# A two-layer decoder's MLPs on one core: M2 behind the whole of M1, product by product over all chunks, and M1's f tiles as half products

## The chip, the core and the metric

One core of a Trainium2 chip runs the whole program. The metric is the device time of one launch in microseconds; a kernel is timed in several runs, and the median counts. The profile is of one further execution, with a span from the first to the last instruction and the busy time of each engine: PE (matmuls), PEld (weight loads of PE), DVE, ACT, POOL, and SP, which only issues DMAs here.

## What is computed

A decoder of two layers on 512 tokens of width 1024, all in float32. Layer 0 mixes by pooling, layer 1 by a gated spatial unit (SGU); both then have the same MLP, which is where the change is:

```python
def sq_relu_mlp(h, w1, w2):
    return jnp.square(jax.nn.relu(h @ w1)) @ w2

for i in range(DEPTH):
    mod = c_act @ ada_w[i] + ada_b[i]
    sh1, sc1, g1, sh2, sc2, g2 = jnp.split(mod, 6, axis=-1)
    h = modulate(rmsnorm(x, norm_mix_g[i]), sh1, sc1)
    ...
    x = x + g1[:, None, :] * y
    h = modulate(rmsnorm(x, norm_mlp_g[i]), sh2, sc2)
    x = x + g2[:, None, :] * sq_relu_mlp(h, mlp_w1[i], mlp_w2[i])
return rmsnorm(x, final_g)
```

`w1` is 1024 x 4096 and `w2` 4096 x 1024. The first product is called M1 here, its 4096 columns are 32 f tiles of 128, four chunks of 8; the second product is M2, and a chunk is 1024 of its contraction rows.

## The kernel before

**Precision.** A float32 operand is split in a high and a low part (`split`, L168, for weights: one ACT copy and one DVE subtract on 128 x 1024; `parts`, L596, for activations). Each product is three matmuls, low x high, high x low and high x high (`mm3`, L180, whose matmul stands in L186). A PE matmul has 128 x 128 weights and 256 or 512 columns.

**Seven for eight.** A product of 2 x 2 blocks is done with seven block products instead of eight, in a form with four accumulators: `ORDER = (1, 5, 6, 3, 7, 2, 4)` names them; 1, 6, 7, 4 go into one accumulator (X), 5 and 3 into another (Z), 2 stands alone. Four of the seven operands on either side are sums of blocks. On the weight side the sums form a chain in one tile: B11, then B12, B22 and B21 are added in turn (`CHAIN`, for products 5, 6 and 4); product 7 takes B12 with B22 added.

**How M1 goes.** In layer 0 a sweep over the eight k tiles (L549 to L575) does 7 f tiles in seven PSUM banks while the activations are still being normed; the other 25 are dense, one `f_run` (L648) each, of 24 matmuls with 512 columns. In layer 1 the first 8 are dense, in halves of 256 tokens, and the other 24 go as `s` units (`s_run`, L730): for each quarter of a chunk pair `(c, j)`, 4 f tiles, seven half products of 24 matmuls with 256 columns. The chain's steps 5 and 6 are added by DVE (L712), step 4 and product 7's block by DMA issued from POOL with an accumulating write (L707). The sums on the activation side are made in four steps by `a_sums` (L662).

**How M2 goes.** Chunks 0 to 2 each take seven products, `p` units (`p_prep` L776, `p_run` L847) of 24 matmuls with 512 columns; every product's banks are evicted and added to y in SBUF by DVE (L867) or copied by ACT. The chain is added by DVE in layer 0 (L790 on, `by_dma` false), by POOL's DMAs in layer 1 (L773). Chunk 3 is dense: eight `q` units (L895) of 24 matmuls.

**The order.** PE's order is written out by hand: a list of units (L913 to L925), in which the p units of chunk c stand between the M1 units of chunk c + 1. Before a unit runs, the operands of some units ahead are prepared (`ahead`, L933). DVE, ACT, POOL and SP get their orders from a scheduler, by the program's order and the buffers. Weight blocks pass through three raw tiles of 4 KB a partition (`w4`) and five pairs of split tiles (`wts`). `extra` spreads the ada tiles over the units: 56 loads of 512 KB with one DVE multiply-and-sum each (L206), which give the modulation of later stages.

**Layer ends.** `gated` (L967) takes a token tile's result into x and sums squares, `normed` (L988) norms two token tiles, turns them on PE (L1000) and splits them. In layer 1, x is written to DRAM (`spill`) and read back through POOL's queue (`reload`, L1017) to make room.

**Matmuls split in columns.** `HEAD` and `TAIL` (L78) split some first or last matmuls of a unit in layer 1 in two column ranges, where s and p units meet. `SHIFT`, `BASE` and `GAP` move tiles by words within 128.

Of the kernel before, what the change touches and what calls it, by code (L numbers as in the profile page):

```python
# [7 lines left out]
F32 = mybir.dt.float32  # L8
# [6 lines left out]
P = 128  # L15
# [11 lines left out]


LINE = 128
SHIFT = {"o": 64, "q": 0, "g": 0}  # L30

BASE = 32
# [45 lines left out]
HEAD = {1: {0: 32}, 5: {0: 64}, 6: {0: 128}, 3: {0: 224}, 4: {0: 128, 1: 128, 2: 128}}  # L78
TAIL = {7: {2: 256}, 2: {2: 448}}


@with_exitstack
def decoder_kernel(ctx: ExitStack, tc: tile.TileContext, xtok, vecs, rows, fgrow, ada0, adag, ada1, pool_w, w1s, w1, w1f, w1b, w2, w2e, w_v, w_u, w_o, wsT, lnp, bs, out):
# [44 lines left out]
    GAP = 16  # L128
    shift(big, BASE - GAP)

    def hparts(gap):
        t = big.tile([P, 2 * KD * S + GAP], F32R, name="hb", tag="hb")
        return t[:, GAP - gap : GAP - gap + 2 * KD * S].rearrange("p (h k s) -> p h k s", h=2, k=KD)

    h_ = [hparts(0)]

    shift(big, LINE - GAP)
    x_ = [big.tile([P, 2, D], F32, name=f"x{h}", tag=f"x{h}") for h in range(2)]
    shift(big, GAP)
    cb = big.tile([P, D], F32, name="cb")  # L140
    gb = big.tile([P, D], F32, name="gb")
# [4 lines left out]
    def H(k, c):  # L146

        return h_[0][:, 0, k, c], h_[0][:, 1, k, c]
# [8 lines left out]
    def raw4(src):  # L157
        r = w4.tile([P, D], F32, name="raw", tag="w4")
        nc.sync.dma_start(r, src)
        return r  # L160
# [51 lines left out]

    dram = ctx.enter_context(tc.tile_pool(name="dram", bufs=1, space=bass.MemoryType.DRAM))
# [10 lines left out]


# [13 lines left out]
    with (  # L239
# [205 lines left out]
        xf = st.tile([P, KD, S], F32, name="xf")  # L445
# [20 lines left out]
        def turned(g):  # L466
            for k in (2 * g, 2 * g + 1):
                A.activation(xf[:, k], pxs.pop(k), AF.Copy)
# [33 lines left out]
        ht, rbs = {}, []  # L502
# [20 lines left out]
        def norm_hi(k):  # L523
            t = ht[k] = st2.tile([P, S], F32, name="ht", tag="ht")
            V.scalar_tensor_tensor(t, xf[:, k], scl[0][1][:, k : k + 1], rbs[0], ALU.mult, ALU.mult)
            A.activation(H(k, ALL)[0], t, AF.Identity, bias=mod(0, c_sh(1, k)))

        def norm_lo(k):
            h, l = H(k, ALL)
            V.scalar_tensor_tensor(l, ht.pop(k), mod(0, c_sh(1, k)), f32(h), ALU.add, ALU.subtract)  # L530
# [20 lines left out]
        for k in range(KD):  # L551
# [12 lines left out]
            else:  # L564
                norm_lo(k)
            (xh, xl), (wh, wl) = H(k, ALL), wk[k][1:]
# [12 lines left out]
    vy = ctx.enter_context(tc.tile_pool(name="vy", bufs=1))  # L579

    def ytile(name):
        return vy.tile([P, NT, D], F32, name=name, tag="y")

# [6 lines left out]

    def parts(o, a):  # L596

        A.activation(o[0], a, AF.Copy)
        V.tensor_tensor(o[1], a, f32(o[0]), ALU.subtract)

    def mlp(i, first, extra, last, ending):

        with (
            tc.tile_pool(name="gq", bufs=3) as gq,
            tc.tile_pool(name="su", bufs=1) as su,
            tc.tile_pool(name="pad0", bufs=1) as pad0,
            tc.tile_pool(name="op", bufs=2) as op,
            tc.tile_pool(name="pad1", bufs=1) as pad1,  # L610
            tc.tile_pool(name="w2p", bufs=3) as w2p,
            tc.tile_pool(name="hx", bufs=1) as hx,
        ):
            shift(pad0, SHIFT["o"])
            shift(pad1, SHIFT["q"] - SHIFT["o"])
            g, y_ = {}, []

            def y(t, dh):
                if not y_:
                    y_.append(ytile("y"))  # L620
                return y_[0][:, t, S * dh : S * dh + S]

            def square(t):
                A.activation(t, t, AF.Square)

            def new_g(c, j):
                g[c, j] = gq.tile([P, 4, S], F32, name="g", tag="g")

            def put(f, po):

                c, q = divmod(f, 8)
                j, p = divmod(q, 4)
                if p == 0:
                    new_g(c, j)
                t = g[c, j][:, p]
                A.activation(t, po, AF.Relu)  # L636
                square(t)

            def quad(c, r, j):

                return g[c, j].rearrange("p a (h r t) -> p a h r t", h=2, r=2)[:, :, :, r]


            def f_prep(u):
                c, f = u
                return split(raw4(w1[8 * c + f] if i == 0 else w1f[8 * c + f]))

            def f_run(u, w):  # L648
                c, f = u
                po = bank("po")  # L650
                wv = w[0].rearrange("p (k c) -> p k c", k=KD), w[1].rearrange("p (k c) -> p k c", k=KD)
                n = 256 if i else S
                for t in range(0, S, n):
                    for k in range(KD):
                        mm3(po[:, t : t + n], cut(wv, ALL, k), H(k, slice(t, t + n)), k == 0, k == KD - 1)
                put(8 * c + f, po)

            sums_a = {}  # L660

            def a_sums(step):  # L662
# [599 lines left out]
```

## Time and profile before

| | us |
|---|---|
| median of 3 runs | 871.62 |
| lowest, highest run | 870.48, 875.11 |
| span of the profiled execution | 867.7 |
| PE busy in it | 854.0 |
| DVE busy | 667.7 |
| ACT busy | 448.4 |
| POOL busy | 49.5 |

The profile's own time is its span; a run's time is measured around the launch. The stages by the chain of waits: loads, ada tiles and the pooling mixer to about 60 us; the sweep to 99; layer 0's M1 and M2 to 395; the SGU to 540; layer 1's M1 and M2 to 858; then the last norm and the output. Groups of the profile's instructions are read as: line, engine, operation, output <- inputs, count | busy us, mean ns of one | idle time before them and what ended it. In the chain, a row is start, length and what it was; `po` is a bank of M1 or the SGU, `pm` of M2, `px` a turned block. For a DMA the row has the issuing queue, count, size and median time from issue to landing; q1 is the queue of plain loads, q0 that of the DMAs issued from POOL.

### The profile page before, as it was taken

To read this page: it belongs to the slowest core of one execution; us is meant where nothing else is said; L and a number is where in the kernel's file an instruction comes from. 1 tells how busy PE (TensorE), PEld (TensorE's weight loads), DVE (VectorE), ACT (ScalarE), POOL (GpSimd) and SP (SyncE) were. 2 spreads that over 40 slices of the span, in tenths; PEclk is the share of its full clock that TensorE was granted. 3 is DMA by queue.
4 is the path that set the end of the run, shared out by engine and by line. 5 is a ranking of instruction groups with operands and counts; after the bars stand their busy time and mean duration, and the time that the engine had idled before them with its cause. 6 is when DMAs were issued, how large, how long until landed. Compare 5 with 4: busy or idle time off the path is not lost.

```text
span 867.7 us, 11816 instructions
## 1 busy us (share of the span) xinstructions
PE 854.0 (98%) x4595; PEld 737.5 (85%) x4595; DVE 667.7 (77%) x884; ACT 448.4 (52%) x653; POOL 49.5 (6%) x69
## 2 busy tenths in 40 slices
PE   8999999999999999999999999999999999999996
PEld 6778888888888888888888888999999998999885
DVE  5889697788869886657799766676687697779855
ACT  4285755454444445238333326665775576566521
POOL 3000000000000000000020001011101000100001
PEclk9999999999999999999999999999999999999999
DMA  9959746454455341605757426937678587668302
GB/s 349 417 217 327 272 172 215 168 181 140 179 205 170 124 168 49 218 27 216 249 186 245 170 74 215 340 75 171 166 240 190 144 232 217 146 147 266 123 24 97
DMA packets 40045, 163.39 MB, mean 188 GB/s; under 512 B 4507, under 2 KB 4659, under 8 KB 34742
## 3 DMA queue, kind: packets, MB, share of 16 engines
q1 hardware_dynamic: 35282, 137.72, 43.8%
q0 software_dynamic: 4560, 24.66, 13.7%
q8 instruction: 36, 0.59, 0.3%
q10 hardware_dynamic: 148, 0.27, 0.1%
q14 instruction: 19, 0.16, 0.1%
HBM read 158.42 MB, written 4.21 MB: 187 GB/s over the span
## 4 chain that ended last, share of the span: by engine, by line
PE 91%; DMA 4%; DVE 2%; ACT 1%; issue 1%; SPq 0%; POOLq 0%; POOL 0%; DVEq 0%; ACTq 0%
PE po L186 52%; PE pm L186 36%; DMA wh<-in_ada 2%; DMA wl<-in_ada 1%; DMA ada<-in_adag 1%; PE po L1104 1%; ACT sq L279 1%; PE px L1000 1%; PE po L570 0%; PE po L573 0%; PE po L571 0%; DVE wl L174 0%; DVE tmp L972 0%; DVE h L1007 0%; PE px L464 0%
## 5 line engine op out<-in xcount | busy, mean ns | idle before, releaser
L186 PE MATMUL po<-hb,wh 128*128 128x256 f32 (+1 forms) x1252 | 298.9, 332 | 0.0
L186 PEld LDWEIGHTS po<-hb,wh 128*128 128x128 f32 x1252 | 211.5, 188 | 23.5
L186 PE MATMUL po<-hb,wl 128*128 128x256 f32 (+2 forms) x632 | 209.0, 333 | 0.4 <-DVE wl L174 0.4
L174 DVE TENSOR_TENSOR wl<-raw,wh 128x1024 fp32r<-128x1024 f32 (+1 forms) x110 | 130.8, 1192 | 41.9 <-ACT wh L173 41.6
L173 ACT ACTIVATE wh<-raw 128x1024 fp32r<-128x1024 f32 (+1 forms) x110 | 113.1, 1034 | 69.8 <-PE pm L186 30.1
L186 PE MATMUL pm<-wh,oh 128*128 128x512 f32 (+2 forms) x342 | 130.9, 386 | 0.0
L186 PE MATMUL pm<-wl,oh 128*128 128x512 f32 x336 | 130.9, 389 | 0.0
L186 PE MATMUL pm<-wh,ol 128*128 128x512 f32 x336 | 130.8, 389 | 0.0
L186 PEld LDWEIGHTS po<-hb,wl 128*128 128x128 f32 x632 | 118.7, 188 | 13.8 <-DVE wl L174 1.0
L174 DVE TENSOR_TENSOR wl<-b,wh 128x1024 fp32r<-128x1024 f32 x60 | 72.6, 1220 | 21.7 <-ACT wh L173 21.7
L206 DVE SCALAR_TENSOR_TENSOR ada<-ada,cb 128x1024 f32<-128x1024 f32 x56 | 68.1, 1219 | 21.8 <-DMA ada<-in_ada 21.6
L186 PEld LDWEIGHTS pm<-wh,oh 128*128 128x128 f32 x342 | 64.2, 188 | 13.5
L186 PEld LDWEIGHTS pm<-wh,ol 128*128 128x128 f32 x336 | 63.1, 188 | 12.5
L186 PEld LDWEIGHTS pm<-wl,oh 128*128 128x128 f32 x336 | 63.1, 188 | 12.3
L173 ACT ACTIVATE wh<-b 128x1024 fp32r<-128x1024 f32 x60 | 63.2, 1056 | 11.6 <-PE pm L186 7.2
L636 ACT ACTIVATE g<-po 128x512 f32<-128x512 f32 x40 | 23.6, 599 | 74.8 <-PE po L186 72.6
L174 DVE TENSOR_TENSOR wl<-bt,wh 128x1024 fp32r<-128x1024 f32 x24 | 29.0, 1222 | 34.4 <-ACT wh L173 34.4
L186 PE MATMUL po<-as,wh 128*128 128x256 f32 x288 | 51.3, 281 | 0.0
L977 ACT ACTIVATE tmp<-x 128x512 f32<-128x512 f32 (+1 forms) x25 | 15.3, 612 | 65.9 <-DVE x L973 65.9
L186 PEld LDWEIGHTS po<-as,wh 128*128 128x128 f32 x288 | 43.9, 189 | 0.0
L867 DVE TENSOR_TENSOR y<-y,pm 128x512 f32<-128x512 f32 x68 | 43.5, 679 | 0.0
L186 PE MATMUL pm<-wh,qo 128*128 128x512 f32 (+1 forms) x144 | 41.1, 366 | 0.0
(203 smaller groups left out, 1302.7 us busy)
## 6 DMA issues: line engine op xcount, KB each, us to landing
ada<-in_ada SPq DMA_DIRECT2D x72, 512.0 KB, 3.8
b<-in_w SPq DMA_DIRECT2D x21, 1024.0 KB, 4.8
raw<-in_w SPq DMA_DIRECT2D x25, 512.0 KB, 4.2
raw<-in_w1b SPq DMA_DIRECT2D x24, 512.0 KB, 5.3
bt<-in_w POOLq DMA_DIRECT2D x9, 1024.0 KB, 8.3
raw<-in_w2e SPq DMA_DIRECT2D x16, 512.0 KB, 3.2
raw<-in_w1b POOLq DMA_DIRECT2D x12, 512.0 KB, 5.3
wh<-in_ada SPq DMA_DIRECT2D x9, 512.0 KB, 9.6
```

The source lines that it names most:

```text
L173: A.activation(h[:, c], r[:, c], AF.Copy)
L174: V.tensor_tensor(l[:, c], r[:, c], f32(h[:, c]), ALU.subtract)
L186: T.matmul(o[:, c], a, b[:, c], start=first and q == 0 and not c.start, stop=last and q == 2 and c.stop is None, **kw)
L206: V.scalar_tensor_tensor(r, r, 1.0, cb, ALU.mult, ALU.mult, accum_out=pmv[i, b][:, j : j + 1])
L279: A.activation(j, X(t)[:, c], AF.Square, scale=D**-0.5, accum_out=out)
L636: A.activation(t, po, AF.Relu)
L867: V.tensor_tensor(yt, yt, banks[hf], ALU.subtract if minus else ALU.add)
L977: A.activation(tmp, xt, AF.Square, scale=D**-0.5, accum_out=s[:, len(cs) : len(cs) + 1])
L1000: T.transpose(px[:, 256 * q + P * r : 256 * q + P * r + P], xs[r][:, P * (k + q) : P * (k + q) + P], ident)
L1104: T.matmul(po[:, tok[t]], vt[t][:, ch, c0 : c0 + P], wb[:, 0, hd], start=True, stop=True)
```

## The change

M1 and M2 of a layer no longer alternate; M2 starts when the whole of M1 is done.

- M1, layer 0: 8 dense f tiles (7 of them in the sweep as before) and chunks 1 to 3, 24 f tiles, as s units. Layer 1: all 32 f tiles as s units.
- M2, both layers: no dense chunk. Product m is done for chunks 0 to 3 before the next product, into the same banks (`start` only at chunk 0, `stop` only at chunk 3); y is touched at chunk 3 alone. Products 3 and 7 take the chunks in pairs.
- M2's chain is added in two pieces of 512 KB by POOL's DMAs in both layers, for products 5, 6, 4 and 7, and a chunk has its own chain tiles. M1's s units keep DVE's two adds and POOL's two.
- The activation sums are made in place in the g tiles (`p_prep`), by DVE, and in layer 0 too now in the h32 tiles (`Sums.step`); the sweep's h32 gets its shift at once (`norm_out`).
- The pools of the MLP are replaced by named slots in one pool (`slot`), reused over the layers: what was g, y, v, u, gt or an ada tile in turn.
- x is written to DRAM in layer 0 as well, and read back on SP's queue behind product 2 of chunk 0.
- Six ada tiles of layer 1 go into layer 0's M1 (with the eight of layer 0's own), ten into its M2, 24 into the SGU, eight into layer 1's M1.
- `HEAD`, `TAIL` and `SHIFT` are gone; `PAD` is new. The last unit is split by token tile, and its last tile in two halves of 256 columns.

```diff
+            for n in range(8):
+                p, hf = (n % 4, n // 4) if end else (n // 2, n % 2)
+                wv = cut(w[p // 2], ALL, slice(S * (p % 2), S * (p % 2) + S))
...
+                mm3(banks[hf], cut(o, ALL, p, hf), wv, start and p == 0, stop and p == 3, skip_group_check=True)
...
+            if c < 3:
+                return
...
+            a = {1: q(0, 0), 5: q(1, 0), 6: q(1, 0), 3: q(0, 0), 7: q(1, 0), 2: q(0, 1), 4: q(1, 1)}[m]
+            if m == 5:
+                minus(a, a, q(1, 1))
+            elif m == 6:
+                minus(a, a, q(0, 0))
+            elif m == 3:
+                V.tensor_tensor(a, q(0, 1), q(1, 0), ALU.add)
+            elif m == 7:
+                V.scalar_tensor_tensor(a, a, -1.0, q(1, 1), ALU.mult, ALU.subtract)
+            o = slot(f"R{c % 2}", [P, 2, 4, 2, P], "o", F32R)
...
+            nxt = {1: CHAIN[5], 5: CHAIN[6], 6: CHAIN[4], 3: (0, 1)}.get(m)
+            w = []
+            for q in range(2):
+                r = raw4(piece(c, 1, 0, q)) if m == 2 else (b2 if m in (3, 7) else ts)[c][q]
+                w.append(split(r))
+                if nxt:
+                    G.dma_start(r, piece(c, *nxt, q), accum_op=ALU.add)
+            if m == 7 and c + 2 < 4:
+                b_load(c + 2)
...
+    def p_units():
+
+        us = [("p", (c, m)) for m in (1, 5, 6) for c in range(4)]
+        us += [("p", u) for u in ((0, 3), (1, 3), (0, 7), (1, 7), (2, 3), (3, 3), (2, 7), (3, 7))]
+        after(us, ("p", (1, 5)), ("bl", (0,)), ("bl", (1,)))
+        us += [("p", (0, 2)), ("xl", (0,)), ("xl", (1,)), ("p", (1, 2)), ("sum", (0, 1)), ("sum", (1, 1)), ("p", (2, 2)), ("p", (3, 2))]
+        us += [("p", (0, 4)), ("sum", (2, 1)), ("sum", (3, 1)), ("p", (1, 4)), ("p", (2, 4)), ("p", (3, 4))]
+        return us
...
+    us = [("cl", (1,)), ("cl", (2,))] + [("put", (f, sweep[f])) for f in (3, 0, 1, 2, 4, 5, 6)] + [("f", 7), ("a", (0,))]
+    us += s_units(1, 0, (1, 2)) + [("a", (1,)), ("sq", (0,)), ("sq", (1,))] + s_units(1, 1, (1, 2)) + [("a", (2,)), ("sq", (2,)), ("sq", (3,))] + s_units(1, 0, (5, 6)) + [("a", (3,)), ("sq", (4,)), ("sq", (5,)), ("sq", (6,))]
+    us += s_units(1, 0, (3, 7)) + s_units(1, 1, (5,)) + s_units(1, 0, (4,)) + s_units(1, 1, (6, 3, 7)) + s_units(2, 0, (1,)) + s_units(1, 1, (4,)) + [("cl", (3,))]
+    us += s_units(2, 0, ORDER[1:]) + s_units(2, 1) + s_units(3, 0) + s_units(3, 1)
+    after(us, ("s", (2, 1, 2)), ("x", spread(0, "gain0")))
```

In the list, `("p", (c, m))` is product m of chunk c, `("s", (c, j, m))` half product m of four f tiles, `bl` loads the block B22 of a chunk, `tl` the chain's B11, `cl` M1's chain, `xl` reads x back, `a` is a step of the activation sums, `put` and `sq` the sweep's Relu and square. Two p units are prepared at a time, the running one and the next; of s units the running one and four more.

888 lines of the change are left out of this document (422 added, 466 removed).

## The prediction

> **What bounds the kernel now.** The page comes first: who is busy, at which clock, and what the chain of waits runs through.
>
> ```profile
> span 867.7 us, 11816 instructions
> PE 854.0 (98%) x4595; PEld 737.5 (85%) x4595; DVE 667.7 (77%) x884; ACT 448.4 (52%) x653; POOL 49.5 (6%) x69
> ...
> PEclk9999999999999999999999999999999999999999
> ...
> q1 hardware_dynamic: 35282, 137.72, 43.8%
> q0 software_dynamic: 4560, 24.66, 13.7%
> ...
> PE 91%; DMA 4%; DVE 2%; ACT 1%; issue 1%; SPq 0%; POOLq 0%; POOL 0%; DVEq 0%; ACTq 0%
> PE po L186 52%; PE pm L186 36%; DMA wh<-in_ada 2%; DMA wl<-in_ada 1%; DMA ada<-in_adag 1%; PE po L1104 1%; ACT sq L279 1%; PE px L1000 1%; PE po L570 0%; PE po L573 0%; PE po L571 0%; DVE wl L174 0%; DVE tmp L972 0%; DVE h L1007 0%; PE px L464 0%
> ```
>
> PE sets the end: 88% of the chain are the matmuls of one helper line, at full clock. So fewer matmul columns are worth their time, as long as the other engines and the DMA keep up. The chain in order of time then gives the price of a matmul, stage by stage.
>
> ```profile
> 95.72 25.16 PE po L186 x111
> 120.88 5.44 PE pm L186 x24
> ...
> 387.60 1.75 PE px L1000 x16
> 389.34 5.46 PE pm L186 x24
> ...
> 547.31 35.38 PE po L186 x312
> 582.69 0.11 PE pb L218
> 582.80 8.48 PE po L186 x72
> ...
> 811.18 46.42 PE pm L186 x216
> 857.60 0.02 issue
> ```
>
> A unit of 24 matmuls of 512 columns takes 5.44 us. Of 256 columns, 312 take 35.38, 113.4 ns each; but behind the one small transpose at 582.69, 72 take 8.48, 117.8 ns each. The same work has a quick and a slow rate. From 582.80 to 811.18 stand 42 half products (2.72 each at the quick rate) and 20 products: 223.0 us, and 228.4 were used, so 5.3 went to the slow rate.
>
> **The change: what PE saves.** Counted in units of 24 matmuls at 512 columns. Layer 0 behind the sweep: now 25 f tiles, 21 products, 8 dense tiles of M2, 54; then 1 f tile, 42 half products (21), 28 products, 50. Layer 1: now 8 + 21 + 21 + 8 = 58; then 56 halves (28) + 28 = 56. Six units less, 6 x 5.44 = 32.6 us. 867.7 - 32.6 = 835.1 if nothing else comes into the way.
>
> The slow rate: 98 half products at (117.8 - 113.4) x 24 = 0.105 us are between 0 and 10.3 us, against 5.3 now. The small transpose moves behind half product 26 of 42 and 41 of 56, so that 31 follow it: 3.3. I take 3.8, as a wait of PE may bring it on too: that is -1.5, with -5.3 and +5 as the ends.
>
> **What hides the rest, engine by engine.** The prices:
>
> ```profile
> L174 DVE TENSOR_TENSOR wl<-b,wh 128x1024 fp32r<-128x1024 f32 x60 | 72.6, 1220 | 21.7 <-ACT wh L173 21.7
> L206 DVE SCALAR_TENSOR_TENSOR ada<-ada,cb 128x1024 f32<-128x1024 f32 x56 | 68.1, 1219 | 21.8 <-DMA ada<-in_ada 21.6
> ...
> L173 ACT ACTIVATE wh<-b 128x1024 fp32r<-128x1024 f32 x60 | 63.2, 1056 | 11.6 <-PE pm L186 7.2
> L636 ACT ACTIVATE g<-po 128x512 f32<-128x512 f32 x40 | 23.6, 599 | 74.8 <-PE po L186 72.6
> ...
> L867 DVE TENSOR_TENSOR y<-y,pm 128x512 f32<-128x512 f32 x68 | 43.5, 679 | 0.0
> ```
>
> Seven half products (19.04 us of PE) need on DVE seven splits, two chain adds and three evictions: 9 x 1.22 + 3 x 0.68 = 13.0 us. Layer 0 has an ada tile to every 2.2 halves too, 3.9: 16.9, so DVE has 2 us to spare in 19. A product (5.44) needs two splits and its operand's low part, 3.66, and 16 of 28 a difference, 1.22. In layer 0 the first twelve products carry 12 x 3.66, all 16 differences and 10 ada tiles: 75.6 us in 65.3 of PE, with some 8 us of lead from the order list and three ada tiles and one difference done before. DVE there is full, late by 0 to 5, but that is the same stretch in which the additions below are late, and the later of two counts, not the sum. The bank chains in return drop the evictions of three chunks in four.
>
> ACT at the head of layer 0: the order of the changed kernel puts between the sweep's last tile and the fifth half product's weights five splits, one operand, 16 Relu and 12 squares of 256 columns. By 1024 columns at 1.06 and 512 at 0.60 a 256 is some 0.38 (an estimate): 6 x 1.06 + 28 x 0.38 = 17.0, begun 2 us before the sweep's end, then DVE 1.2. Due is 5.44 + 4 x 2.72 = 16.3 behind the sweep: nothing. The sixth wants two operands, five squares and its own split more, 5.8 in a gap of 2.72: 3 late. The ends are 0 and 6; I take 4.5, the seventh's operand included. Layer 1's head is the same step behind the second half's norm, without the Relus: 0 to 5, 2 taken. The norm between the layers now has two token tiles at once and a loaded DVE: 1. The tail has the same operations as before, with tile 2 done 2.72 us before the end instead of 5.44: 0.5. Together with the rate: 4.5 + 2 + 1 + 0.5 - 1.5 = 6.5.
>
> **The additions by DMA.** This is the term that decides. POOL adds a block of B into the chain by DMA; layer 0 of M2 had DVE do it, and layer 1 had two half products between two products.
>
> ```profile
> bt<-in_w POOLq DMA_DIRECT2D x9, 1024.0 KB, 8.3
> ...
> raw<-in_w1b POOLq DMA_DIRECT2D x12, 512.0 KB, 5.3
> ...
> xd<-x POOLq DMA_DIRECT2D x2, 1024.0 KB, 6.9
> x<-xd POOLq DMA_DIRECT2D x2, 1024.0 KB, 7.3
> ```
>
> ```profile
> core 0: us, PE busy (x) PEld busy (x) DVE busy (x) ACT busy (x) POOL busy (x), PEclk, DMA share, GB/s
> 582.80:660.70 77.90, 77.90 (x513) 71.18 (x512) 58.04 (x56) 51.13 (x66) 7.13 (x9) 1.00 0.71 190
> 660.70:738.70 78.00, 78.00 (x517) 71.39 (x515) 61.10 (x62) 48.72 (x60) 6.81 (x8) 1.00 0.73 189
> ```
>
> What 1 MB of addition costs of all 16 DMA engines: at least 5.05 us (q0 has 13.7% of 867.7 = 118.9 us for 24.66 MB, some of it plain); at most 6.0 (from 512 KB to 1 MB the landing grows from 5.3 to 8.3). A plain 512 KB costs 1.45 (q1: 43.8%, 380 us for 137.72 MB). In 660.70:738.70 POOL issued 6 MB of additions beside 16 plain halves: 0.73 x 78.0 = 56.9, less 23.2, leaves 5.6 a MB. I take 5.35, between the floor and this.
>
> In M2 each unit now asks for 1 MB of addition: four units, 21.8 us of PE, want 21.4 us of the engines before any plain load. Due dates: what is added behind (c,1), (c,5), (c,6) is read four units later or much later still; but the block that (0,3) leaves behind is read by (0,7), two units on, and twelve additions stand ahead of it in POOL's queue. From its first weights, 6 us ahead of M2, until (0,7), unit 14, the engines must move 13 MB of additions, and in layer 0 some 15 plain halves (4 chain blocks, 7 ada, 4 of B22): 13 x 5.35 + 15 x 1.45 = 91.3, landed 85.3 after M2's start. ACT and DVE then take 1.06 + 2 x 1.22 = 3.6: 88.9, and due was 14 x 5.44 = 76.2. Layer 0 stands 12.7 us. Layer 1 has no ada tiles there, 9 plain halves: 69.6 + 13.1 - 6 + 3.6 = 80.2, 4.0 late. Behind (0,7) the queue is empty enough. The wait is ACT's, at the split of (0,7); behind it in ACT's and DVE's order are that unit's operand and all later splits, behind those POOL's next additions, and PE waits for the lot. Sum 16.7; at 5.05 the two are 8.8 and 0.1, at 6.0 21.2 and 12.5.
>
> Three moved steps cost nothing by these rows. x now goes out in layer 0 too, 2 MB during the sweep, and comes back in SP's queue instead of POOL's, 7.3 us, asked for by the splits at units 18 and 19 and wanted at 21; behind it in that queue stand the second blocks of (1,2), which land in time if x does, and cost up to 3 us if not. The sweep has eight more ACT copies of 0.60 in 38 us. And POOL issues 8 additions in 21.8 us at some 0.8 each (7.13 us for 9 instructions in the first window), 6.4 of 21.8.
>
> [...]
>
> **Sum.** 835.1 + 6.5 + 16.7 = 858.3 of span. The profiled span of 867.7 lies 3.9 us under the median of the runs, 871.62; with those, **862 us**.
>
> **The rivals.** (a) The forecast: M2 stands at (0,7), longer in layer 0. Own range 854 to 871. 0.45.
>
> (b) The queue is hidden: the additions overlap better than the shares say, or the lead is longer. For it: no wait of the chain before names q0. Against: 0.73 of DMA share with half as dense a stream. 835.1 + 6.5 + 3.9 = 845.5; at the quick rate throughout 842. 0.22.
>
> (c) Slower: the additions bind through. The two stalls together are 26p - 122.4 for a price p per MB, 6.5 us of work being fixed. From p = 5.71 the gain is gone, from 5.88 the kernel is over 0.5% slower. For it: 6.0 between the two landings, and that waiting in a row leaves gaps. Against: 5.6 was reached with the row above. At 6.0: 845.5 + 33.7 = 879. 0.20.
>
> (d) All half products run at the slow rate, for the columns that steadied the matmuls behind a product are no longer split off: 5 us on top of (a) and some more standing, 868. For it: the 8.48. Against: 312 matmuls in a row at the quick rate. 0.10. [...]
>
> The rest, 0.03, is a wait that I have not seen, as a load behind a slot that comes free late.
>
> **From there to the numbers.** Less than 0.5% (4.4 us) can't be told from no change here. Faster than 867.3: of (a) 0.32, (b) 0.22, (d) 0.04: 0.58. Within: 0.13 + 0.05 + 0.05 of (a), (c), (d): 0.23. Slower: 0.19. The range runs from the quick end of (b) to just under (c) at 6.0: 843 to 878.
>
> **What would show it.** PE's busy time falls by some 32 us, and M2's products stand in a row at 5.44. If I am right, the waits list a DMA addition ahead of the splits of (0,7), at the fifteenth product, with PE idle behind it for about 13 us in layer 0 and 4 in layer 1, DMA share over 0.9 for the 70 us before. (b) shows no idle PE there; (c) idle already at (2,6) and in layer 1 as long as in layer 0; (d) rows of half products at 2.82 instead of 2.72 a unit. Idle PE at the first half products behind the sweep would be ACT's Relus. I am wrong if the time is lost elsewhere: in DVE's differences and ada tiles in M2, in half products that wait for their raw blocks, or in a turn from one layer to the next.

## The result, and the profile after

The changed kernel takes 893.46 us in the median of four runs (888.57 to 896.06), beside 871.05 us of the kernel before: a ratio of 1.0245, 95% interval 1.0202 to 1.0287. It is slower, by more than twice what the forecast of 862 us was to win against 871.62, and it lies outside the range of 843 to 878.

The profile is of the slowest of the four runs, 896.06 us. Its page, the same parts as were shown of before: span and busy time, the granted clock and the DMA share in 40 slices, the two queues (packets, MB, share of 16 engines), and the first row of the chain of waits.

```profile
span 894.4 us, 12710 instructions
PE 845.1 (94%) x4895; PEld 738.2 (83%) x4895; DVE 693.5 (78%) x886; ACT 512.2 (57%) x732; POOL 110.5 (12%) x137
...
PEclk9999999999969999999999999999999999999998
DMA  9989969876999988336658864557566799998411
...
q1 hardware_dynamic: 37090, 133.52, 41.9%
q0 software_dynamic: 14352, 54.02, 31.4%
...
PE 51%; DVE 20%; DMA 17%; ACT 5%; issue 4%; POOL 1%; SPq 1%; POOLq 0%; DVEq 0%; ACTq 0%
```

Two numbers of the second row split the difference. PE was busy 854.0 of 867.7 before and is busy 845.1 of 894.4 now: its idle time grew from 13.7 to 49.3, by 35.6. With 32.6 us of matmuls taken away its busy time should be 821.4; it is 23.7 more, so the matmuls that are left take longer. 35.6 + 23.7 - 32.6 = 26.7, the whole difference of the spans. One slice of the clock shows a 6, and the share of PE in the chain fell from 91% to 51%. The forecast had counted 24.7 us of new idle time, and 1.5 us less for the matmuls than those 821.4.

Where PE stands is in the view of its waits: engine, line, releaser, us in total, times, the longest.

```profile
PE pm L194 <- DVE o L634: 13.0, 1, 13.0
PE b201q L194 <- DVE g L776: 3.1, 1, 3.1
...
PE b011q L194 <- ACT g L770: 2.7, 1, 2.7
PE b311q L194 <- DVE g L776: 2.6, 1, 2.6
PE b101q L194 <- ACT g L770: 2.6, 2, 2.3
PE po L194 <- DVE wl L182: 2.5, 1, 2.5
...
PE b012q L194 <- ACT h L969: 2.0, 1, 2.0
```

There is one wait of 13.0 us in M2 of layer 0 (`pm`) and none of this kind in layer 1. Six waits are of 2.0 to 3.1 us, five of them at banks of M1's half products (the names carry chunk and quarter: `b201q` is chunk 2, quarter 0). In the kernel before, PE has no gap over 0.25 us from 56 us on. For the long one the chain goes back from PE to an ada tile's load; DVE's and SP's rows beside it (start, length; in brackets the idle time before and what ended it) say why.

```profile
237.63 24.80 DMA ada<-in_ada
...
263.68 1.15 DVE o L634
...
264.88 10.23 PE pm L194 x36
```

```profile
245.95 0.15 DVE L203 SCALAR_TENSOR_TENSOR scl<-mods,vec 128x1 f32<-128x1 f32 x1
260.38 1.23 DVE L214 SCALAR_TENSOR_TENSOR ada<-ada,cb 128x1024 f32<-128x1024 f32 x1 [14.28 <-DMA ada<-in_ada]
...
234.78 2.27 SPq L804 DMA_DIRECT2D b<-in_w  x4
237.14 5.72 SPq L210 DMA_DIRECT2D ada<-in_ada  x3
```

M2 begins at 235.3. SP issues four loads of B22 (`b`), 2 MB that product 3 needs 65 us later, and behind them three ada tiles. DVE reaches an ada tile's multiply-and-sum at 246 and stands there 14.28 us, then at the next one until 262.45. The low part of the operand of product 1 of chunk 2 (`o`, L634) comes behind both in DVE's order, and PE waits for that. For this kind of load the page's median from issue to landing is 4.7 us:

```profile
ada<-in_ada SPq DMA_DIRECT2D x72, 512.0 KB, 4.7
```

The load that the chain names took 24.80. In the stretch the DMA engines are full, by the windows (us, busy time by engine, granted clock, DMA share, GB/s):

```profile
240.00:250.00 10.00, 10.00 (x46) 8.19 (x45) 5.56 (x8) 5.88 (x6) 2.54 (x3) 1.00 1.06 275
250.00:255.00 5.00, 1.91 (x9) 1.23 (x7) 0.00 (x0) 2.26 (x3) 0.00 (x0) 0.97 1.05 274
255.00:260.00 5.00, 0.00 (x0) 0.00 (x0) 0.00 (x0) 0.00 (x0) 0.00 (x0) 0.50 1.06 277
260.00:265.00 5.00, 0.12 (x1) 0.13 (x1) 3.78 (x6) 0.00 (x0) 0.00 (x0) 0.50 0.81 306
265.00:270.00 5.00, 5.00 (x15) 4.01 (x16) 5.00 (x8) 0.46 (x1) 1.71 (x2) 0.67 0.68 163
```

The DMA share is 1.06 from 255 to 260 us, while PE, DVE and ACT do nothing: loads and additions are both under way, with q1 at 42.8% and q0 at 57.3% of the 16 engines' time from 235 to 266. The granted clock, the last column but two, is the second finding. PE stands from 251.9 to 264.9 us, and the clock is halved from 254.7 to 268.4.

The rate of the matmuls is the third. The chain's rows of layer 1:

```profile
723.71 2.83 PE b311q L194 x24
726.54 131.62 PE pm L194 x564
```

564 matmuls of 512 columns in 131.62 us are 233.4 ns each, with no wait and at full clock; 226.7 (5.44 us a unit) was counted on. Half products take 2.83 a unit here, the slow rate known from before.

### The profile page after: what moved, and what is told of

Same layout as the page of the kernel before. It is cut to its first block, busy times and chain, and to the rows that moved or that the text cites. A ratio compares the mean times of both kernels' runs of the same rounds, so it can differ in the third digit from the quotient of the medians.

```text
span 894.4 us, 12710 instructions
## 1 busy us (share of the span) xinstructions
PE 845.1 (94%) x4895; PEld 738.2 (83%) x4895; DVE 693.5 (78%) x886; ACT 512.2 (57%) x732; POOL 110.5 (12%) x137
## 3 DMA queue, kind: packets, MB, share of 16 engines
q0 software_dynamic: 14352, 54.02, 31.4%
## 4 chain that ended last, share of the span: by engine, by line
PE 51%; DVE 20%; DMA 17%; ACT 5%; issue 4%; POOL 1%; SPq 1%; POOLq 0%; DVEq 0%; ACTq 0%
PE pm L194 29%; DMA ada<-in_ada 7%; DVE wl L182 5%; DVE ada L214 3%; PE po L194 3%; PE b211q L194 2%; PE b301q L194 2%; DMA wh<-in_ada 2%; PE b311q L194 2%; DMA ch10q<-in_w1b 2%; PE b201q L194 2%; ACT wh L181 2%; DVE ada L393 1%; PE b101q L194 1%; PE b111q L194 1%
## 5 line engine op out<-in xcount | busy, mean ns | idle before, releaser
L194 PE MATMUL pm<-wh,o 128*128 128x512 f32 (+1 forms) x904 | 284.4, 396 | 13.5 <-DVE o L634 13.0
L194 PEld LDWEIGHTS pm<-wh,o 128*128 128x128 f32 x904 | 171.1, 190 | 53.1 <-DVE o L634 13.4
L194 PE MATMUL pm<-wl,o 128*128 128x512 f32 (+1 forms) x452 | 179.1, 396 | 1.1 <-DVE wl L182 1.1
L634 DVE TENSOR_TENSOR o<-g,o 128x1024 fp32r<-128x1024 f32 x56 | 68.5, 1224 | 44.8 <-ACT o L633 44.6
L194 PEld LDWEIGHTS pm<-wl,o 128*128 128x128 f32 x452 | 85.8, 190 | 21.2 <-ACT tmp L935 1.5
L633 ACT ACTIVATE o<-g 128x1024 fp32r<-128x1024 f32 x56 | 59.3, 1058 | 71.5 <-PE pm L194 69.7
L181 ACT ACTIVATE wh<-bt 128x1024 fp32r<-128x1024 f32 x64 | 67.3, 1054 | 32.9 <-PE pm L194 32.3
L182 DVE TENSOR_TENSOR wl<-bt,wh 128x1024 fp32r<-128x1024 f32 x64 | 78.5, 1236 | 5.2 <-ACT wh L181 5.1
L194 PE MATMUL po<-hb,wh 128*128 128x512 f32 x224 | 70.4, 395 | 0.0
L194 PEld LDWEIGHTS po<-hb,wh 128*128 128x128 f32 x224 | 42.1, 188 | 9.9
L780 ACT ACTIVATE g<-g 128x512 f32<-128x512 f32 x42 | 26.1, 622 | 20.1 <-DVE g L774 12.9
```

The source lines that it names most:

```text
L181: A.activation(h[:, c], r[:, c], AF.Copy)
L182: V.tensor_tensor(l[:, c], r[:, c], f32(h[:, c]), ALU.subtract)
L194: T.matmul(o[:, c], a, b[:, c], start=first and q == 0 and not c.start, stop=last and q == 2 and c.stop is None, **kw)
L780: A.activation(t, t, AF.Relu)
```

## The experiments

Fifteen kernels, most of them the changed kernel with one edit. "Span" is that of the profiled execution; ratios are to the kernel before, with their interval.

**e1: B22's loads held back.** The loads wait for a small copy that reads a later operand.

```diff
+            if c < 2 and i == 0:
+                A.activation(t[:, :, 0:1], f32(last_o[0][:, 0, 0:2, 0, 0:1]), AF.Copy)
...
-        after(us, ("p", (1, 5)), ("bl", (0,)), ("bl", (1,)))
+        after(us, ("p", (1, 6)), ("bl", (0,)), ("bl", (1,)))
```

> The loads of B22 for chunks 0 and 1 (4 x 512 KB) are held back until the operand of product 5 or 6 is split, so that layer 0's last ada tiles stand ahead of them in SP's queue. All work is kept. Theory A (the 13 us of idle PE at product 1 of chunk 2 in layer 0 come from DVE standing at an ada tile whose load is behind those four loads): that stall falls to under 3 us and its half-clock tail with it, span 894 to 880 to 884, and no new stall over 3 us. Theory B (the predicted one: POOL's additions need the time anyway, so a stall only moves): PE stands at (0,3) or (0,7) of layer 0 instead, 6 to 13 us, span 888 to 895.

Measured: 885.02 us, ratio 1.0159 (1.0144 to 1.0174), span 882.0. The wait of 13 us is gone, and two of 2.0 and 2.6 us have come, at product 3 of chunks 0 and 1, for the loads that were held. Both theories are half right. The order of the loads decided who stood, and 8.4 of the median's 22 us went with it; but the DMA engines stay at a share of 1.04 to 1.07 from 236 to 316, and now the held loads are late. With all bytes and additions as before, the waits in this stage come to 4.6 us in place of 13.0, and none is at (0,7).

**e2: no ada tiles in layer 0's M2** (ten loads and multiply-and-sums left out).

```diff
-        us.insert(at + 1, ("x", lambda q=q: ada_tile(1, q, ada1[8 + q], get4)))
+        us.insert(at + 1, ("x", lambda q=q: ada_none(1, q)))
```

> The ten ada tiles in layer 0's M2 are left out (loads and multiply-and-sums; their columns of the modulation get a constant), so the numbers computed differ. Theory A: the stall at (2,1) goes with all of its 13 us and the half clock behind it, span 894 to 878 to 882; M1's waits of layer 0 and all of layer 1 stay as they are. Theory B: 5 MB less of plain loads (14.5 us of the DMA engines by 1.45 us a half MB) would take away a stall at (0,7) only if there were one; the stall at (2,1), before which 3 to 4 MB of additions are queued, keeps 6 us or more, span 884 to 890.

Measured: 873.42 us, ratio 1.0024 (0.9998 to 1.0050), span 871.1: 20 us less. M2 of layer 0 has no wait in it at all. That is more than theory A gave: with 5 MB of loads out of the way no other load is late either, and the wait of 2.6 us at `b311q`, at the end of M1, is gone too, where DVE had the first of these ada tiles ahead of an eviction. All additions are still there, and the DMA share stays at 1.05 to 1.06 from 230 to 300: full DMA engines alone do not make PE wait.

**e6: no additions in layer 0's M2**, the complement (B22's loads and the ada tiles stay).

```diff
-                if nxt:
+                if nxt and i:
```

> Layer 0's M2 issues no additions (28 of 512 KB left out: the chain's tiles and B12 keep what they held, so the numbers differ); the loads of B22 and the ada tiles stay as they are, in their order. Theory A1 (ada tiles behind B22's loads, for which the additions are only slow company): the four loads and the ada tiles are 2 MB and up to 3 tiles at 2.9 us a MB, so the stall at (2,1) is still 2 to 5 us. Theory B1 (the additions fill the DMA engines, and whoever waits for a load waits for them; the predicted price, another place): no wait over 1 us in all of layer 0's M2, DMA share under 0.7 there, span 13 to 17 us less.

Measured: 878.03 us, ratio 1.0078 (1.0051 to 1.0104), span 874.6: 15.4 us less. Theory B1's case in full, by the windows of its M2:

```profile
236.00:266.00 30.00, 30.00 (x133) 24.61 (x132) 29.34 (x39) 18.43 (x20) 0.00 (x0) 1.00 0.52 183
266.00:296.00 30.00, 30.00 (x133) 24.62 (x132) 28.80 (x26) 17.50 (x18) 0.00 (x0) 1.00 0.00 1
296.00:326.00 30.00, 30.00 (x133) 24.62 (x132) 19.51 (x17) 18.44 (x19) 0.00 (x0) 1.00 0.22 71
```

PE is never idle there, and the share falls from over 1 to 0.52 and to nothing. The same four loads and ada tiles in the same order cost DVE 0.2 us of waiting in M2 and PE none when the additions are gone. The additions fill the DMA engines, as forecast, and DVE at its ada tile was the one who was caught: the wait needs both, since it also goes when the ada tiles are left out (e2). (By the trace 32 pieces were left out, 16 MB, and not 28.)

**e3 and e4: where the tiles stand.** e3 moves all SBUF tiles up by 64 bytes. e4 moves what lies between two paddings by 192 bytes, the tiles of split weights among it.

```diff
 e3
+    shift(big, 16)
     h_ = hparts(["P0", "P1", "P2", "P3"])
 e4
-PAD = 112
+PAD = 64
...
-    shift(big, 16)
+    shift(big, 64)
```

> One shift of 16 words ahead of the first tile: all SBUF tiles move up by 64 bytes, so that the moving operands of M1 stand at 192 modulo 512 and the weights' tiles at 256, as in the kernel before. Nothing else changes. Theory C (the slow matmul rate, 5.60 instead of 5.44 us for 24 matmuls of 512 columns and 4.90 instead of 4.76 a sweep step, is set by where tiles stand): the sweep goes back to 4.76 a step and at least M1's and the SGU's units to 5.44, span 6 to 20 us less. Theory D (the rate is a state that PE falls into, and stays in, whatever the addresses): the rates stay as in the changed kernel, or change without a pattern, span within 3 us.

> The tiles of split weights move to 384 modulo 512, where the operands stand at 128: in M2 the moving weights are 256 bytes from the stationary operand's residue, as in the kernel before (256 against 0). Nothing else changes. Theory C, as a matter of the distance between the two: M2's units go to 5.44 (28 x 2 x 0.16 = 9 us less), M1's may go either way by up to 5 us. Theory D: within 3 us.

Measured: 891.85 us, 1.0260 (1.0226 to 1.0295), and 893.40 us, 1.0255 (1.0220 to 1.0289). Neither is faster, and the totals would end the theory; the rows don't. In e3 no stage gets the rate of before back: the sweep stays at 233.3 ns a matmul, M2 runs at 228.9 in layer 0 and 233.3 in layer 1. In e4 every stage with 512 columns, sweep, M2 and SGU, runs at about 226.8 ns, the rate of the kernel before; and all half products run at 120.0 ns, worse than either rate known so far. The gain in one kind of matmul was paid for by the other.

**e5: M2's operand alone at that distance.**

```diff
+OFF = 80
...
-            o = slot(f"R{c % 2}", [P, 2, 4, 2, P], "o", F32R)
+            o = slot(f"R{c % 2}", [P, 2 * D + LINE], "o", F32R)[:, OFF : OFF + 2 * D].rearrange(...)
```

> Only M2's operand tiles o move, to 448 modulo 512, 256 bytes from the weights' tiles at 192; everything else stays where the changed kernel has it. Theory C2 (the rate of matmuls of 512 columns follows the distance of the two operands' tiles modulo 512: 64 gives 233, 256 gives 227 ns, as e4 showed for all units together): M2's units go from 5.60 to 5.44, 28 x 2 x 0.16 = 9.0 us less, all other stages keep their rates, ratio to before about 1.015. Theory D (a state that PE is in, that e4 met by chance): no change beyond 3 us, or a change in the sweep and the SGU too.

Measured: 888.20 us, ratio 1.0194 (1.0168 to 1.0220), span 888.4: 5.3 us less. The row of M2 in layer 1, to be held against the 131.62 us of the changed kernel:

```profile
724.34 127.88 PE pm L196 x564
```

The starts are 226.7 ns apart in all of M2; sweep and SGU keep their rates. Theory C2, not D, as far as this distance goes. Of the 9.0 us the two stages of M2 show 6.8 in the profiles (174.9 to 171.9 us in layer 0, 159.0 to 155.2 in layer 1). The first units of layer 0 ran at 229 ns in the changed kernel already, and that stage of e5 has 2.0 us more of PE's work at half clock. The medians, 5.3 us apart, are of runs whose rates are not known one by one (see e14).

**e9 and e10: four more distances**, two in each run, by chunk parity.

```diff
+OFF = (16, 112)   # e10: (48, 96)
...
+            o = slot(f"R{c % 2}", [P, 2 * D + LINE], ...)[:, OFF[c % 2] : OFF[c % 2] + 2 * D]...
```

> The weights' tiles stay at 192 modulo 512. M2's operand o stands at 192 for even chunks (distance 0) and at 64 for odd ones (distance 128); M1's sums of products 6 and 3 likewise. Read from the rows: ns from one matmul to the next, unit by unit. Theory C2 (the distance of the two tiles sets the rate): each chunk of M2 has one rate in both layers, as far as 256 gave 226.7 and 64 gave 229 or 233; even and odd chunks may differ. Theory D: the rate doesn't follow the chunk.

> As the run before, with o at 320 for even chunks (distance 128 to the other side, 384) and at 0 for odd ones (distance 192); M1's sums of products 6 and 3 likewise. Theory C2: one rate for each chunk parity, in both layers; and the half products' rate (113.4, 117.8 or 120.0) changes with product 6 and 3 against the others. Theory D: no such pattern.

Measured: one run each, 891.23 and 893.58 us. Two units of e9 in layer 1, the rows of its `wl` matmuls (every third):

```profile
758.76 0.39 PE L196 MATMUL pm<-wl,o 128*128 128x512 f32 x1
759.44 0.39 PE L196 MATMUL pm<-wl,o 128*128 128x512 f32 x1
760.12 0.39 PE L196 MATMUL pm<-wl,o 128*128 128x512 f32 x1
...
764.27 0.39 PE L196 MATMUL pm<-wl,o 128*128 128x512 f32 x1
764.96 0.40 PE L196 MATMUL pm<-wl,o 128*128 128x512 f32 x1
765.67 0.39 PE L196 MATMUL pm<-wl,o 128*128 128x512 f32 x1
```

0.68 for three matmuls in one unit, 0.69 and 0.71 in the next, and so in turn through both layers. Averaged over units, ns a matmul by the weights' tile against the operand's, modulo 512 bytes: 0: 227.4; 64: 229.0 or 233.3; 128: 232.9; 192: 232.9; 256: 226.7; 384: 232.4. Those at 0, 128, 192 and 384 are from one run each. Theory C2 as far as M2 goes.

**e11: the kernel before with M2's operand 64 bytes off.**

```diff
-SHIFT = {"o": 64, "q": 0, "g": 0}
+SHIFT = {"o": 112, "q": 0, "g": 0}
```

> The kernel BEFORE, with the shift of M2's operand tiles changed so that they stand 64 bytes from the weights' residue, as in the changed kernel, instead of 256. Theory C2: its 42 products of M2 and 4 of the dense units that read these tiles go from 226.7 to 229 to 233.3 ns a matmul, 46 x 24 x (2.3 to 6.6) = 2.5 to 7.3 us more, and the phases of the half products beside them may change by up to 3 us more. Theory D: no change.

Measured: 872.43 us, ratio 1.0026 (1.0012 to 1.0039): slower by little, at the lower bound of what C2 gave. Its M2 runs at 229.0 ns a matmul in place of 226.7. The worse rate of that distance, 233.3, which the changed kernel has, comes in four units only.

**e7: no ada tiles in layer 0's M1** (fourteen left out).

```diff
-    ex = [lambda q=q: ada_tile(0, 40 + q, ada1[q], ada_slot(q)) for q in range(8)]
-    ex += [lambda q=q: ada_tile(1, q, ada1[8 + q], ada_slot(q)) for q in range(EX)]
+    ex = [lambda q=q: ada_none(0, 40 + q) for q in range(8)]
+    ex += [lambda q=q: ada_none(1, q) for q in range(EX)]
```

> The fourteen ada tiles in layer 0's M1 are left out (loads and multiply-and-sums; constants in their place, so the numbers differ). Theory E (DVE stands at ada tiles whose loads are late, and the evictions behind them make PE wait): the four waits of layer 0's M1, 7.1 us, and the half clock behind two of them are gone, M1 of layer 0 takes 128.2 - 9 to 11 us, span 882 to 886. Theory F (the half products themselves want too much of DVE, or of the raw tiles): 3 us or more of waits stay, span 887 to 892. The stall at (2,1) of M2 stays in both.

Measured: 885.24 us, ratio 1.0161 (1.0136 to 1.0185), span 885.1: 8.2 us less. In layer 0's M1 the waits at `b111q` and `b201q` (0.6 and 3.1 us) and the larger one at `b101q` (0.9) are gone; that at `b311q` stays with 2.0 us, behind the first ada tiles of M2 (it is gone in e2). Theory E. The half products are not too much for DVE; DVE is made to stand at tiles whose loads are late.

**e8: half product 4 one unit later in layer 1's M1.**

```diff
-        us += s_units(c, j, (5,) if c < 2 else (1,))
+        us += s_units(c, j, (5, 6) if c < 2 else (1, 5))
...
-        us += s_units(c, j, (6, 3, 7) if c < 2 else ORDER[1:])
+        us += s_units(c, j, (3, 7) if c < 2 else ORDER[2:])
```

> In layer 1's M1 the half product 4 of a quarter is done one unit later, behind product 6 of the next quarter (5 of the next where that is the order), so that the chain's last addition has 2.7 us more to land. Theory G (ACT stands at the split of the chain for product 4, 4.7 and 5.0 us by the trace, because the addition by DMA takes 8 to 10 us to land, and the evictions behind that split are late): the waits of 2.7 and 2.3 us at two X banks are gone and with them the half clock behind them, span 4 to 9 us less. Rival: it is the loads of raw tiles, or the banks, and the waits only move: within 2 us.

The rows of the changed kernel on which theory G rests, POOL's issue and ACT's order at one of the two waits:

```profile
601.02 0.85 POOL L738 DMA_DIRECT2D ch01q<-in_w1b  x1 [0.65 <-DVE wl L182]
...
609.22 1.06 ACT L181 ACTIVATE wh<-ch01q 128x1024 fp32r<-128x1024 f32 x1 [4.69 <-DMA ch01q<-in_w1b]
610.18 0.58 ACT L770 ACTIVATE g<-b011q 128x512 f32<-128x512 f32 x1
```

An addition that lands 8.2 us after its issue holds ACT for 4.69 us at a split; the eviction of a bank that PE waits for is the next instruction. Measured: 890.23 us, ratio 1.0224 (1.0202 to 1.0245): 3.2 us less, just under what theory G gave, and no more than the changed kernel's own runs differ by (888.57 to 896.06), so that the rows have to carry the reading. The two waits behind evictions by ACT are gone; one of 2.0 us for a split's low part is new. The half clock that theory G counted on stood behind neither wait: the granted clock is 1.00 from 606 to 630 us.

**e14: one matmul split in two places of the slow row.**

```diff
+                    two = {0: 128} if i and u in ((2, 0, 6), (3, 0, 6)) and f + k == 0 else {}
```

> The changed kernel with one matmul of 256 columns done as two of 128 at the start of half product 6 of quarters (2,0) and (3,0) in layer 1. Theory H (the two rates of half products are two phases of the same row of matmuls, and anything that shifts one matmul can turn the one into the other): the stretch that ran at 117.8 ns from 638 us on in the changed kernel changes to 113.4 at one of the two places, up to 42 x 0.105 = 4 us less. Theory I (what stands beside, such as writes by DMA or evictions, sets the rate): no change at these places.

Measured: 890.93 us in one run. Its chain, from the small transpose (`pb`) over the second split (25 matmuls in place of 24):

```profile
679.82 2.72 PE b212q L194 x24
682.54 0.11 PE pb L235
682.65 2.83 PE b211q L194 x24
...
691.14 2.85 PE b301q L194 x25
693.99 2.72 PE b305q L194 x24
...
723.91 129.11 PE pm L194 x564
```

2.72 us a unit ahead of the transpose, 2.83 behind it, and 2.72 again from the split to the end of M1, where the changed kernel has 2.83. Theory H at the second place; at the first the row was quick already, and stayed so. In no other profiled run with these tiles does the row turn between the transpose and the end of M1.

The last row shows more than was asked. M2 of layer 1 follows on M1, and its 564 matmuls take 129.11 us here, 228.9 ns each, with the very tiles that gave 131.62 in the changed kernel; nothing in M2 was edited. So the 233.3 of the changed kernel is a phase too. In the nine profiled runs with its distances between tiles, M2 of layer 1 runs at 229.0 where M1's last half products were quick (e1, e2, e14) and at 233.3 where they were slow (the changed kernel, e3, e6, e7, e8, e15). Of the 3.7 us between 131.62 and e5's 127.88, 2.5 are this phase and 1.2 the distance. A single profile of these kernels can be some 2.5 us longer or shorter by it in layer 1's M2 alone, whatever was edited.

**e15: PE kept busy in the long wait**, by 45 matmuls of constants.

```diff
+            if i == 0 and u == (2, 1):
+                dm = bank("dm")
+                for _ in range(45):
+                    T.matmul(dm[:, 0:P], ones, ident, start=True, stop=True)
```

> The changed kernel with 45 matmuls of constants (128 x 128, float32, some 0.21 us each, 9.6 us in all) put on PE ahead of product 1 of chunk 2 in layer 0, where PE waits 13 us; their result is read by nobody. Theory J (the clock is halved because PE was idle): the granted clock stays 1.00 from 250 to 275 us, and product 1 of chunk 2 takes 5.5 to 5.6 us instead of 7.2 to 7.4; the wait shrinks to about 3 us and what is left may still halve one stretch of 3.4 us. Theory K (what runs beside PE halves it): the clock is 0.50 there as before, and the constants' matmuls take twice their time.

The windows, to be held against those of the changed kernel above:

```profile
255.00:260.00 5.00, 5.00 (x48) 5.00 (x47) 0.00 (x0) 0.00 (x0) 0.00 (x0) 1.00 1.06 276
260.00:265.00 5.00, 5.00 (x24) 4.07 (x23) 1.34 (x3) 1.06 (x1) 0.00 (x0) 1.00 0.91 311
265.00:270.00 5.00, 3.42 (x16) 2.48 (x15) 4.96 (x11) 2.01 (x2) 0.85 (x1) 1.00 0.61 207
```

The clock stays at 1.00 with the same DMA traffic beside it, and the wait shrinks to 1.6 us. Theory J. One run gave 894.44 us: M2 of layer 0 is 5.0 us shorter than in the changed kernel, partly by the phase of its matmuls, and the stages ahead of it are 3.6 longer, with longer waits in M1.

**e12 and e13: the parts together, with all work.** e12 has e1, e5 and e8, and the multiply-and-sums of layer 0's ada tiles read a column of ones that ACT writes from a later result, so that DVE comes to them later. e13 takes e1 out again, moves the ten tiles behind product 3, and does the spread of the gain's row later.

```diff
 e12
-        V.scalar_tensor_tensor(r, r, 1.0, cb, ALU.mult, ALU.mult, ...)
+            A.activation(one, gate, AF.Identity, bias=ones[:, 0:1], scale=0.0)
+            V.scalar_tensor_tensor(r, r, one, cb, ALU.mult, ALU.mult, ...)
 e13
-    at = us.index(("p", (1, 5)))
+    at = us.index(("p", (0, 3)))
```

> The changed kernel with all its work, and four things mended: B22's loads held back (e1, a little less long), o at 448 (e5), half product 4 a unit later in layer 1 (e8), and the multiply-and-sums of layer 0's ada tiles made to wait, each on a result two units later, so that DVE doesn't stand at them. If the parts add up (8.4 + 5.3 + 3.2 + 4 to 8 of the median 893.5): 868 to 873. If they share one limit, the DMA engines in layer 0's M2, which a faster PE meets earlier: 874 to 880. Under the kernel before only if nearly all add up.

> As e12, but B22's loads go where the changed kernel has them, the ten ada tiles of layer 0's M2 follow product 3 of chunk 0 one by one (the engines were busy 0.3 to 0.75 of the time from there on in e12), and the gain's row is spread 11 half products later. Same work, same bytes. Theory B1 as a matter of place (additions fill the DMA engines only for the first 80 us of M2): no wait over 2 us in layer 0's M2, and no 4 us at the small transpose, 881.9 - 12 - 6 for the waits and the half clock behind them: 861 to 868, under the kernel before. Theory B2 (the layer's bytes don't fit as such): waits come back behind (0,7), 872 to 880.

Measured: e12 881.86 us, ratio 1.0128 (1.0107 to 1.0150), above both forecasts; the parts don't add up. DVE still stood at ada tiles in M2, and PE with it, 7.8 us at product 6 of chunk 3, because B22's loads were ahead of the last ones again, and the small transpose of the gain's row waited 4.1 us for the delayed ada tiles of M1, a cost of this mending. e13: 877.99 us (873.95 to 883.94), ratio 1.0090 (1.0060 to 1.0121). Its M2 has no wait for the first 98 us, all of them at a DMA share near 1; behind that, six waits of 5.9 us together, at product 7, whose blocks land late, and at product 2, whose blocks share the raw tiles with the ada tiles. By its time and by the place of its waits, behind (0,7), this is theory B2; but the waits are small, the longest 2.0 us, so that the place of the loads was worth more than their bytes. What keeps e13 above the kernel before was not taken apart further. No version here beats the kernel before.

## Why the prediction was wrong

**What PE saves: the step that failed.** "A unit of 24 matmuls of 512 columns takes 5.44 us" was carried over from rows of the kernel before, and PE's full clock with it. Busy time was forecast at 821.4 - 1.5 and measured at 845.1: 25.2 of the 36.1 us between 858.3 and the span of 894.4. It has two parts, the clock and the rates. In the windows that cover the stretches at half clock

```profile
169.30:172.80 3.50, 3.50 (x19) 3.50 (x19) 3.50 (x6) 3.47 (x6) 0.00 (x0) 0.51 0.79 234
230.80:234.20 3.40, 3.32 (x15) 3.32 (x16) 3.40 (x6) 2.67 (x4) 0.85 (x1) 0.50 1.06 235
254.70:268.40 13.70, 3.52 (x8) 2.81 (x9) 7.18 (x12) 0.00 (x0) 1.71 (x2) 0.50 0.84 257
534.60:538.00 3.40, 3.40 (x9) 2.52 (x8) 3.40 (x5) 0.04 (x1) 0.00 (x0) 0.50 0.76 272
572.10:575.60 3.50, 3.50 (x19) 3.50 (x18) 2.61 (x4) 2.44 (x5) 0.00 (x0) 0.51 0.90 194
```

PE was busy 17.2 us, of which half, 8.6, is lost; e15 shows for the longest of these waits that PE's idle time brings it on (1.00 in place of 0.50). So they cost more than their length, which the sum didn't have. The rates are the other 16.6, or 15.1 against the rates of before, since the forecast had put 1.5 less. M2's 56 units, nearly all at 233.3 ns, cost 0.16 us too much each against e5's, some 8 to 9 us; what is left is sweep, SGU and half products. By e14 and e5, two thirds of that 0.16 are a phase of the row and one third the distance between tiles. The diff said that `SHIFT` was gone and `PAD` new, and the prediction passed over it: the terms of the sum took the duration of an instruction as a property of its shape.

**Idle time that the sum put at nothing** makes the other 10.9 us. Of the 24.7 that were forecast, 20.1 came: 13.0 for the additions (16.7 forecast) and 7.1 for heads, norm and tail (8.0). Waits that the sum did not have come to 14.5: 7.1 at banks of half products in M1 of layer 0, 4.9 in M1 of layer 1, 2.5 in the SGU; 1.0 is in the first 55 us. M1's are answered below, by e7 and e8; the SGU's was not tried.

**The slow rate of half products** (rival (d), and 3.8 us in the forecast). The 98 half products were neither all quick nor all slow: there are long stretches of either (113.3 and 117.8 ns a matmul), that begin and end at waits, at the small transpose, or (e14) at a split matmul. About half were slow, an estimate of 5 us from the rows, so the term's size was near. Its reason was not: the transpose does not make the row slow, it can turn it either way (quick to slow in e3 and e8, slow to quick in e1 and e2). For (d), e14 shows that a split matmul can turn the row; that the split ones of before steadied it was not tried. The 5.3 us that the prediction read as the slow rate in the kernel before also hold these splits: in its chain two half products take 5.46 us as 48 matmuls and 5.56 to 5.84 as 49.

**The additions by DMA.** The mechanism was right, the place wrong. The price: q0 took 31.4% of 894.4 us for 54.02 MB, and in e6, with 16 additions of 1024 KB left out, 22.0% of 874.6 for 37.24 MB. The difference, 88.4 us, is 5.5 us for each 1024 KB, forecast 5.35. The total in layer 0: 12.7 forecast, 13.0 of idle PE measured, and e6 shows that without additions there is none. But the due date that was missed first was not that of (0,7). The ada tiles, B22's four blocks and four of the chain's stood in the sum as fifteen plain halves, bytes without a due date. The sum did not ask who waits for them: DVE does, in order, 10 us into M2. During the wait at (2,1) POOL issued no addition for 19 us. What (0,7) reads was issued at 309.93 and 311.96 and was there when ACT split it at 318.58 and 319.94. That the two sizes agree is luck: with the same bytes and additions, e1 loses 4.6 us in this stage and e13 5.9, and in neither does PE stand at (0,7). In layer 1 the DMA engines are as full for the first 65 us, and PE never waits in M2 until the last units:

```profile
735.00:800.00 65.00, 65.00 (x280) 52.66 (x279) 54.18 (x47) 38.75 (x41) 18.79 (x22) 1.00 1.05 210
800.00:865.00 65.00, 65.00 (x281) 52.63 (x280) 48.66 (x48) 38.02 (x44) 3.41 (x4) 1.00 0.50 138
```

4.0 forecast, 0 measured; 14 units at 5.60 instead of 5.44 gave the queue 2 us more by (0,7), which may be part of it; the rest was not tried.

**Rival (c)** ended on the right side for the wrong reason: additions at 6.0 us a MB were to bind through both layers; the price was 5.5, and layer 1 had no such wait.

**ACT at the heads, the norm, the tail** (8.0 together). At the head of layer 0's M1 PE waited 1.3 us for ACT (4.5 forecast), at that of layer 1 2.4 (2 forecast), in the norm between the layers 1.7 (1), in the tail 1.7 (0.5): together 7.1, near enough. DVE's 16.9 us of work in 19 was a sum of durations, and right as such; but in M1 of layer 0 it stood at ada tiles whose loads were late (e7: 8.2 us with what follows), and in layer 1 ACT stood at additions that took 8.2 and 10.0 us to land instead of 5.3 (e8, by its rows). The list of what would make the forecast wrong had the ada tiles in M2 in it, and the raw blocks, and gave them 0.03 of the chance.

## What to carry to other kernels

A load in a queue needs a name for whoever waits for it first; on an engine that works in order, work with no hurry of its own (here the ada tiles, at one of which DVE stood 14.28 us, and PE 13.0 behind it) sets the due date of everything behind it, so load it before the rush or place it where the DMA engines have time. Take the duration of a matmul from a row only together with the places of its tiles and with what ran ahead of it: when a change moves tiles or order, the rate is a term of its own, with a range (here 226.7 to 233.3 ns for 512 columns). And count a wait of PE as possibly longer than it is: in the changed kernel five waits of 2.0 to 13.0 us had 17.2 us of matmuls at half clock around or behind them, 8.6 us lost; two of 2.3 and 2.7 us had none.

## What the runs showed of the hardware

**In these kernels the rate of the float32r matmuls changed with where the two operands' tiles stand to one another.** In M2, a matmul of 512 columns takes 226.7 ns at a distance of 256 bytes modulo 512 (e4, e5, e12, e13), 227.4 at 0, and 229 to 233.3 at 64, 128, 192 and 384. Half products, with 256 columns, have it the other way round: 120.0 ns at 256 (e4), against 113.3 or 117.8 at 64. The distance alone does not account for every rate: the sweep of before runs at 226.7 with its tiles 64 bytes apart, and the changed kernel's at 233.3; e3, which gave it the very residues of before, left it there. What else differs there (the high and low parts stood 16 KB apart and now stand 4 KB apart) wasn't tried alone.

**A row of matmuls had phases.** With the same tiles and the same shape, 113.3 and 117.8 ns follow one another in stretches of tens of us, and in one run a single matmul split in two turned one into the other. With 512 columns at a distance of 64 bytes the two are 229.0 and 233.3; in layer 1 the phase at M1's end went on through all of M2 in nine runs of nine.

**The clock was halved in stretches of 3.41 us, or a whole multiple.** In the changed kernel they begin at 169.35, 230.79, 254.69 (four times as long, 13.65 us), 534.58 and 572.13 us, during a wait of PE or up to 1.3 us after it (3.1, 2.6, 13.0, 2.5 and 2.0 us long), and reach into the work behind: PE was busy 17.2 us in the windows that cover them. Waits of 2.7 and 2.3 us, which ended at 611 and 627 us, had none, so that the length alone doesn't decide. In this trace all changes of the clock from 169.35 us on lie on a grid of 3.413 us. PE's idle time, added up by step of this grid, sorts the cases: each of the six steps at full clock with more than 2.0 us of idle PE (2.02 to 3.41, the last of them at the end, when PE has no more work) was followed by one at half clock; of those with less than 1.8 us none was. The wait of 2.7 us lies across two steps, 1.55 us of idle time in the one and 1.14 in the other; of that of 2.3 us, 1.77 lie in one step; that of 2.0 us, 2.02, lies within one. So a wait's place on the grid counted in this trace, beside its length.

**Loads and additions in competition.** At the start of layer 0's M2, with the DMA share at 1.05 to 1.06 (240 to 260 us), a 512 KB load of an ada tile, 4.7 us in the median of the whole run from issue to landing, took up to 24.8; in e6, with no additions beside them in that stage, the longest took 10.0, and PE waited for none of them in M2.
